# mLSTM values: which two of the four weight pages are split into the page pool and which two into the ring, exchanged

## The chip, the core and the metric

The kernel runs on one NeuronCore of a Trainium2 chip. The metric is the device time of one execution in microseconds; before the change it was 1633.11 us, the median of 3 runs (1631.96 to 1634.64). TensorE (PE) does the matmuls, VectorE (DVE), ScalarE (ACT) and GpSimd (POOL) the element work, and SyncE (SP) issues nearly all DMAs. Each engine works through its own instructions in the order in which the program put them, and waits on semaphores for the others.

## The reference

One decoder layer of 1024 rows and width 1024: three token mixers beside each other (stick-breaking attention, an mLSTM, cross-attention into 256 memory rows), a gated merge, and a ConvFFN. What the change touches is one column block of the input projection, the mLSTM's values (512 columns, `ml_v`):

```python
h = _rmsnorm(x, g_mix[l])
(sb_q, sb_k, sb_v, ml_q, ml_k, ml_v, ml_o, ml_i, ml_f, xa_q, gate_pre) = jnp.split(
    h @ w_in[l], offsets, axis=-1)
y_sb = _merge_heads(_stick_breaking_attention(
    _split_heads(sb_q, SB_HEADS), _split_heads(sb_k, SB_HEADS), _split_heads(sb_v, SB_HEADS)))
...
num = (jnp.einsum('bhts,bhsd->bhtd', s, vc)
       + w_inter[..., None] * jnp.einsum('bhvk,bhtk->bhtv', c_st, qc))
```

Here `vc` is one 128-row chunk of `ml_v`. All in fp32.

## The kernel before

**Products in three.** A product of fp32 operands is made of three matmuls of a faster format (`mm3`, lines 142, 143, 144): each operand is split into a high part, rounded by ACT (line 129), and a low part, the rest, subtracted on DVE (line 130). `wsplit` does this for a weight page of 128x1024: it loads the page into a `raw` tile by a DMA from SP (line 135) and splits it into two tiles, `hi` and `lo`.

**Where tiles live.** Tiles come from pools with a fixed number of slots for each tag; a new tile takes a slot over, and its first writer waits for the last reader of the tile that had it. Here these matter: `raw` (2 slots), `whi` and `wlo` (2 slots each, called the ring here), `pg` (16 slots, the page pool), and in PSUM the banks `pj`, `pv`, `z` and `tr`. A split goes into the ring unless `wsplit` is given another tag.

**The mLSTM's values.** `nat_chunks(1, ...)` makes eight tiles of 128 rows and 512 columns, each a sum over eight blocks k of the normalised input `hh`/`hl` (tiles `h`, the stationary operand) and four weight pages (the moving operand): page b serves k = 2b and 2b + 1, so a tile takes six matmuls for each of the pages 0, 1, 2, 3, in this order. All four pages are split once and stay for the eight tiles. Before, pages 0 and 1 lie in the ring and pages 2 and 3 in the page pool. The same generator makes the stick-breaking values (`which` 0): there it is given two pages that were split earlier (`ws=early`).

**What runs around it.** The stick-breaking attention goes over four pairs of heads p, each in twelve pieces: scores on PE (`sb_weights`, lines 394 and 395, bank `z`), two sigmoids on ACT (397, 398), a mask on POOL (403), scans on DVE (408) and a product (410); then transposes on PE (`sb_turn`, line 420, bank `tr`) with a copy on ACT (424 or 428), and products with the values (`sb_apply`, line 440, bank `pv`). Between the pieces PE runs chunks of a projection: those of the next pair's queries and keys while p < 3, and the mLSTM's values while p = 3. The queries and keys of a pair are six `pg` tiles, which are free when the pair's last scores are done. Behind the values come the gated projections (`seven`), whose weights are split in halves into `wlo` and `whi` in turn (`qring`), while `gx_part` makes their other operands, twelve `pg` tiles, from loads of `hn_d`.

**What sets the order.** The tile framework orders each engine's instructions by the program's order and by priorities; `tc.high_priority` in `nat_chunks` puts the loads and splits of the pages forward by a fixed offset (`SOON`), and what a slot's former reader allows decides where they land. So an exchange of slots moves rows on several engines.

Of the kernel before, what the change touches and what calls it, by code (L numbers as in the profile page):

```python
# [42 lines left out]
def tile_hybrid_layer(ctx: ExitStack, tc: tile.TileContext, xT, memT, vecs, w_t, w_n, w_kv, w_if,  # L43
# [24 lines left out]
    def T(shape, tag, dt=F32, bufs=None):  # L68
        pool = {"mw": mlp, "mst": mlp, "px": late[0], "sx": late[0]}.get(tag, sb)
        return pool.tile(shape, dt, tag=tag, name=nm(tag), bufs=bufs or BUFS[tag])  # L70
# [18 lines left out]
    def bank(tag):  # L89
        if tag in ("pj", "pv"):  # L90
            return ps.tile([P, HALF], F32, tag=tag, name=nm("ps_" + tag), bufs=2)
        if px1 is not None:
            if not spare.get(tag):
                t = two(tag)
                spare[tag] = [t[:, 1], t[:, 0]]
            return spare[tag].pop()
        return psx[0].tile([P, HALF], F32, tag=tag, name=nm("ps_" + tag), bufs=2)
# [4 lines left out]
    def hs(h):  # L102
        return slice(h * HALF, (h + 1) * HALF)

    def ts(t):
        return slice(t * P, (t + 1) * P)
# [21 lines left out]
    def split(src, hi, lo, eng=None):  # L128
        nc.scalar.activation(hi, src, AF.Copy)  # L129
        (eng or nc.vector).tensor_sub(lo, src, hi.bitcast(F32))  # L130

    def wsplit(src, tag=None, eng=None, raw=None):
        if raw is None:
            raw = T([P, S], "raw")
            nc.sync.dma_start(raw, src)
        hi = T([P, S], tag or "whi", F32R)
        lo = T([P, S], tag or "wlo", F32R)
        split(raw, hi, lo, eng)
        return hi, lo

    def mm3(out, lh, ll, rh, rl, start, stop, more=False):
        nc.tensor.matmul(out, lh, rh, start=start, stop=False, skip_group_check=more)  # L142
        nc.tensor.matmul(out, lh, rl, start=False, stop=False, skip_group_check=more)  # L143
        return nc.tensor.matmul(out, ll, rh, start=False, stop=stop, skip_group_check=more)  # L144
# [185 lines left out]

    def nat_chunks(which, consume, order=range(NCH - 1, -1, -1), ws=(), pauses=(3,)):
        with tc.high_priority(offset=SOON):
            ws = list(ws) + [wsplit(w_n[which, b], None if b < 2 or ws else "pg") for b in range(len(ws), 4)]
        for t in order:
            p = bank("pj")
            for k in range(KT):
                wh, wl = ws[k // 2]
                mm3(p, hh[k][:, ts(t)], hl[k][:, ts(t)], wh[:, hs(k % 2)], wl[:, hs(k % 2)],
                    k == 0, k == KT - 1)
                if k in pauses:  # L340
                    yield
            consume(t, p)
            yield
# [202 lines left out]
    def ev_sbv(t, p):  # L546
        if t % 2:
            sbv[t // 2] = T([P, 2, HALF], "pg")
        nc.scalar.activation(sbv[t // 2][:, t % 2, :], p, AF.Copy)

    vals = nat_chunks(0, ev_sbv, ws=early)
    for _ in range(2):
        next(vals)
# [46 lines left out]
    for p in range(4):  # L600
        now = st
        if p < 3:
            st, chunks = sb_qk(p + 1)
            chunks = itertools.chain(own, chunks())
            own = ()
        else:
            chunks = nat_chunks(1, ev_v, [0, 1, 2, 3, 7, 6, 5, 4], pauses=(1, 3, 5))
        for n, (rb, o) in enumerate(PIECES):
            g = sb_weights(p, now, rb, o)
            if len(turned) == 4:  # L610
                apply_all()
            if len(weights) == 2:
                turn_next()
            weights.append((p, rb, o, g))
            for _ in range((FIRST if p == 0 else NEXT)[n]):
                next(chunks, None)
        if p < 3:
            for _ in chunks:
                pass
# [470 lines left out]
    ws = [[None, None] for _ in range(4)]  # L1090
# [33 lines left out]
    for i in range(3 * KT):  # L1124
        b, n = i // KT, ORDER[i % KT]
# [512 lines left out]
```

## Time and profile before

| | us |
|---|---|
| median of the runs | 1633.11 |
| the profiled execution, its whole time | 1633.01 |
| its span (first to last instruction) | 1631.3 |
| granted TensorE clock, mean | 1.00 |
| mLSTM values, first to last matmul of theirs | 254.8 to 330.3 |

The timings of rows are from the profiled execution, counted from the start of the span; the whole time has 1.7 us more, which lie outside it. A row of the timeline gives start, duration, engine, line, operation, output and inputs with shapes, and in brackets how long the engine was idle before it and for whom; buffer numbers are left out there. PE's matmuls are pipelined, so that records overlap and a duration is longer than the step to the next start.

### The profile page before, as it was taken

To read this page: it belongs to the slowest core of one execution; us is meant where nothing else is said; L and a number is where in the kernel's file an instruction comes from. 1 tells how busy PE (TensorE), PEld (TensorE's weight loads), DVE (VectorE), ACT (ScalarE), POOL (GpSimd) and SP (SyncE) were. 2 spreads that over 40 slices of the span, in tenths; PEclk is the share of its full clock that TensorE was granted. 3 is DMA by queue.
4 is the path that set the end of the run, shared out by engine and by line. 5 is a ranking of instruction groups with operands and counts; after the bars stand their busy time and mean duration, and the time that the engine had idled before them with its cause. 6 is when DMAs were issued, how large, how long until landed. Compare 5 with 4: busy or idle time off the path is not lost.

```text
span 1631.3 us, 21183 instructions
## 1 busy us (share of the span) xinstructions
PE 1613.9 (99%) x7959; PEld 1322.4 (81%) x7959; DVE 1226.2 (75%) x1674; ACT 835.5 (51%) x1281; POOL 103.6 (6%) x175
## 2 busy tenths in 40 slices
PE   8999999999999999999999999999999999999999
PEld 4878888888878888888878888788888888888887
DVE  5658888859764666766586989987787777889764
ACT  4557777545554454656411456655555455543431
POOL 1022222020000010100000001100000000000000
PEclk9999999999999999999999999999999999999999
DMA  8420111324324665434884334432222221576131
GB/s 285 170 60 27 40 40 66 136 85 148 126 105 143 198 188 178 136 110 141 314 299 147 125 123 110 129 104 71 78 96 94 83 78 52 196 294 245 45 136 72
DMA packets 102082, 215.06 MB, mean 132 GB/s; under 512 B 13336, under 2 KB 37208, under 8 KB 101980
## 3 DMA queue, kind: packets, MB, share of 16 engines
q1 hardware_dynamic: 100396, 210.82, 38.1%
q0 software_dynamic: 1584, 2.88, 1.1%
q8 instruction: 63, 1.03, 0.3%
q14 instruction: 39, 0.32, 0.1%
HBM read 159.07 MB, written 54.61 MB: 131 GB/s over the span
## 4 chain that ended last, share of the span: by engine, by line
PE 92%; DMA 3%; DVE 3%; ACT 1%; issue 1%; SPq 0%; POOL 0%; DVEq 0%; ACTq 0%
PE ps_pj L142 13%; PE ps_pj L144 13%; PE ps_pj L143 13%; PE ps_pv L144 5%; PE ps_pv L142 5%; PE ps_pv L143 5%; PE ps_z L142 4%; PE ps_z L144 4%; PE ps_z L143 4%; PE ps_tr L142 4%; PE ps_tr L143 4%; PE ps_tr L144 4%; PE ps_pv L440 2%; PE ps_tr L420 2%; PE ps_z L215 1%; PE ps_z L395 1%
## 5 line engine op out<-in xcount | busy, mean ns | idle before, releaser
L143 PE MATMUL ps_pj<-h,whi 128*128 128x512 f32 x516 | 201.7, 391 | 0.0
L142 PE MATMUL ps_pj<-h,whi 128*128 128x512 f32 x436 | 173.9, 399 | 0.6 <-DVE U L1143 0.5
L129 ACT ACTIVATE whi<-raw 128x512 fp32r<-128x512 f32 (+1 forms) x99 | 81.2, 821 | 171.3 <-PE ps_pj L143 75.4
L144 PE MATMUL ps_pj<-h,wlo 128*128 128x512 f32 x352 | 137.6, 391 | 0.1
L848 DVE SCALAR_TENSOR_TENSOR y<-U,vec,y 128x1023 f32<-128x1023 f32 x88 | 112.6, 1280 | 8.4 <-ACT y L846 8.3
L143 PEld LDWEIGHTS ps_pj<-h,whi 128*128 128x128 f32 x516 | 97.1, 188 | 18.9 <-DVE U L276 0.2
L408 DVE TENSOR_TENSOR_SCAN U<-U 128x512 f32<-128x512 f32 (+3 forms) x96 | 92.8, 1009 | 22.1 <-POOL U L403 20.5
L142 PE MATMUL ps_pj<-pg,whi 128*128 128x512 f32 x268 | 104.7, 391 | 0.0
L144 PE MATMUL ps_pj<-pg,wlo 128*128 128x512 f32 x248 | 96.8, 390 | 0.0
L142 PEld LDWEIGHTS ps_pj<-h,whi 128*128 128x128 f32 x436 | 82.0, 188 | 17.6 <-issue 1.1
L144 PEld LDWEIGHTS ps_pj<-h,wlo 128*128 128x128 f32 x352 | 66.1, 188 | 14.7 <-DVE wlo L130 0.6
L129 ACT ACTIVATE whi<-pg 128x512 fp32r<-128x512 f32 (+1 forms) x54 | 43.7, 811 | 66.8 <-PE ps_z L143 18.7
L143 PE MATMUL ps_pv<-h,whi 128*128 128x512 f32 x190 | 74.0, 390 | 0.0
L143 PE MATMUL ps_pj<-pg,whi 128*128 128x512 f32 x188 | 73.4, 391 | 0.0
L130 DVE TENSOR_TENSOR wlo<-raw,whi 128x1024 fp32r<-128x1024 f32 x44 | 53.8, 1222 | 18.0 <-ACT whi L129 18.0
L846 ACT ACTIVATE y<-U,vec 128x1024 f32<-128x1024 f32 x44 | 54.6, 1242 | 20.4 <-DVE U L739 16.7
L144 PE MATMUL ps_pj<-h,whi 128*128 128x512 f32 x156 | 60.8, 390 | 0.0
L144 PE MATMUL ps_pv<-h,wlo 128*128 128x512 f32 x152 | 59.7, 392 | 0.0
L142 PE MATMUL ps_pv<-h,whi 128*128 128x512 f32 x150 | 59.0, 393 | 0.5 <-DVE U L739 0.5
L142 PEld LDWEIGHTS ps_pj<-pg,whi 128*128 128x128 f32 x268 | 50.3, 188 | 10.2
L144 PE MATMUL ps_tr<-pg,wlo 128*128 128x512 f32 x144 | 56.1, 389 | 0.0
L130 DVE TENSOR_TENSOR wlo<-raw,wlo 128x512 fp32r<-128x512 f32 x53 | 36.5, 688 | 26.0 <-ACT wlo L129 25.8
(508 smaller groups left out, 4485.8 us busy)
## 6 DMA issues: line engine op xcount, KB each, us to landing
raw<-in_w_t_dram SPq DMA_DIRECT2D x29, 512.0 KB
gate_d<-U SPq DMA_DIRECT2D x24, 512.0 KB
U<-gate_d SPq DMA_DIRECT2D x22, 512.0 KB
act_d<-y SPq DMA_DIRECT2D x22, 512.0 KB
pg<-in_w_t_dram SPq DMA_DIRECT2D x21, 512.0 KB
raw<-in_w_dn_dram SPq DMA_DIRECT2D x18, 512.0 KB
h<-act_d SPq DMA_DIRECT2D x14, 512.0 KB
raw<-in_w_br_dram SPq DMA_DIRECT2D x12, 512.0 KB
```

Source lines behind the costliest of these rows:

```text
L129: nc.scalar.activation(hi, src, AF.Copy)
L130: (eng or nc.vector).tensor_sub(lo, src, hi.bitcast(F32))
L142: nc.tensor.matmul(out, lh, rh, start=start, stop=False, skip_group_check=more)
L143: nc.tensor.matmul(out, lh, rl, start=False, stop=False, skip_group_check=more)
L144: return nc.tensor.matmul(out, ll, rh, start=False, stop=stop, skip_group_check=more)
L215: nc.tensor.matmul(pm[m], mg[k // 4][:, c], w[:, hs(kk)], start=(k == 0), stop=(k == KT - 1))
L395: nc.tensor.matmul(z[:, a, :w], qs[a][:, ts(rb)], kz[a][:, c], start=False, stop=True)
L408: nc.vector.tensor_tensor_scan(f[:, a, 1:w + 1], f[:, a, 1:w + 1], f[:, a, 1:w + 1], 1.0 if o == 0 else f[:, a, 0:1], op0=ALU.mult, op1=AL ...
L420: nc.tensor.transpose(pt[:, a, ts(j)], g[:, a, ts(j)], ident)
L440: nc.tensor.matmul(pv[64 * a:64 * a + 64, ts(rb % 4)], sbv[s // 2][:, s % 2, (2 * p + a) * 64:(2 * p + a + 1) * 64], wt[a][:, ts(j)], star ...
L846: nc.scalar.activation(out, u, AF.Identity, bias=bias, scale=taps[0])
L848: nc.vector.scalar_tensor_tensor(out[:, :S - s], u[:, s:], taps[s], out[:, :S - s], op0=ALU.mult, op1=ALU.add)
```

## The change

```diff
     def nat_chunks(which, consume, order=range(NCH - 1, -1, -1), ws=(), pauses=(3,)):
         with tc.high_priority(offset=SOON):
-            ws = list(ws) + [wsplit(w_n[which, b], None if b < 2 or ws else "pg") for b in range(len(ws), 4)]
+            ws = list(ws) + [wsplit(w_n[which, b], None if b > 1 else "pg") for b in range(len(ws), 4)]
```

For the mLSTM's values (no page given) pages 0 and 1 now go to the page pool and pages 2 and 3 to the ring. For the stick-breaking values, where b is only 2 and 3, both lines say the ring. No instruction is added or removed; the number of matmuls, splits and loads is the same.

The order of instructions changes on PE, DVE, ACT and SP; POOL's stays. In the rows below a tile's name ends in its number: `2426`/`2427` are the high and low part of page 0, `2432`/`2433` of page 1, `2438`/`2439` of page 2, `2444`/`2445` of page 3; `ps_pj_2448` is the first tile of values, `ps_z_2394` and `ps_z_2461` are the scores of the first two pieces of the last pair, and `xN` counts equal rows.

TensorE, at the start of the values, before:

```order
L395 MATMUL ps_z_2394<-pg_1871,pg_1867 128x128
L420 MATMUL ps_tr_2411<-ident,U_2313 128x128 x8
L142 MATMUL ps_pj_2448<-whi_2426,h_94 128x512
L143 MATMUL ps_pj_2448<-wlo_2427,h_94 128x512
L144 MATMUL ps_pj_2448<-whi_2426,h_102 128x512
L142 MATMUL ps_pj_2448<-whi_2426,h_95 128x512
L143 MATMUL ps_pj_2448<-wlo_2427,h_95 128x512
L144 MATMUL ps_pj_2448<-whi_2426,h_103 128x512
L142 MATMUL ps_pj_2448<-whi_2432,h_96 128x512
L143 MATMUL ps_pj_2448<-wlo_2433,h_96 128x512
```

The same place on TensorE now:

```order
L395 MATMUL ps_z_2394<-pg_1871,pg_1867 128x128
L142 MATMUL ps_pj_2448<-pg_2426,h_94 128x512
L440 MATMUL ps_pv_2324<-y_2356,pg_766 64x128 x2
L440 MATMUL ps_pv_2324<-y_2356,pg_636 64x128 x3
L420 MATMUL ps_tr_2411<-ident,U_2313 128x128 x8
L440 MATMUL ps_pv_2324<-y_2356,pg_636 64x128
L143 MATMUL ps_pj_2448<-pg_2427,h_94 128x512
L144 MATMUL ps_pj_2448<-pg_2426,h_102 128x512
L142 MATMUL ps_pj_2448<-pg_2426,h_95 128x512
L143 MATMUL ps_pj_2448<-pg_2427,h_95 128x512
L144 MATMUL ps_pj_2448<-pg_2426,h_103 128x512
L142 MATMUL ps_pj_2448<-pg_2432,h_96 128x512
```

Six products of the attention (L440) have come forward, one value matmul stands ahead of the eight transposes where none did, and the matmul on page 0's low part (2427) stands behind them. Further on the rest of the thirty products stands in five more groups between the value matmuls, scores and transposes; before they stood in two groups around the scores `ps_z_2495` (128x384), the third piece. The two lists of TensorE are alike again from `ps_z_2550` (the fourth piece) and the transposes behind it on, but for the tags of the pages.

DVE, the splits of the pages among the attention's work, before (from the scans and product of `U_2364` on):

```order
L408 SCALAR_TENSOR_TENSOR U_2363<-U_2363 128x512 x2
L410 TENSOR_TENSOR U_2364<-U_2364,U_2363 128x1024
L130 TENSOR_TENSOR wlo_2433<-raw_2430,whi_2432 128x1024
L130 TENSOR_TENSOR pg_2439<-raw_2436,pg_2438 128x1024
L368 TENSOR_TENSOR pg_1870<-ps_pj_2268,pg_1868 64x512
```

And now:

```order
L408 SCALAR_TENSOR_TENSOR U_2363<-U_2363 128x512 x2
L410 TENSOR_TENSOR U_2364<-U_2364,U_2363 128x1024
L130 TENSOR_TENSOR pg_2427<-raw_2424,pg_2426 128x1024
L130 TENSOR_TENSOR pg_2433<-raw_2430,pg_2432 128x1024
L368 TENSOR_TENSOR pg_1870<-ps_pj_2268,pg_1868 64x512
```

The low part of page 0 was made some twenty rows earlier before; now it has page 1's place, page 1 has page 2's, and page 2 stands five rows further down, behind the scans of `U_2466`, with page 3 two rows behind it. On ACT the high parts follow suit: page 0's behind the second sigmoid of `U_2364` and ahead of the two copies of line 428, page 1's among the copies of the keys (364 to 367), pages 2 and 3 around the second sigmoid of `U_2467`. On SP the load of page 2 (`raw_2436`), which takes over page 0's raw slot, is moved behind a store of the attention's output.

DVE at the end of the values, where the weights of the first gated projection (`raw_3158`) are split into the ring; `pg_3019` is one of the operands that `gx_part` makes. Before:

```order
L795 TENSOR_TENSOR U_3096<-U_3096,U_3095 128x1024
L130 TENSOR_TENSOR wlo_3164<-raw_3158,wlo_3164 128x512
L130 TENSOR_TENSOR whi_3181<-raw_3158,whi_3181 128x512
L130 TENSOR_TENSOR pg_3019<-U_3096,pg_3018 128x1024
L130 TENSOR_TENSOR wlo_3207<-raw_3201,wlo_3207 128x512
```

And now:

```order
L795 TENSOR_TENSOR U_3096<-U_3096,U_3095 128x1024
L130 TENSOR_TENSOR pg_3019<-U_3096,pg_3018 128x1024
L130 TENSOR_TENSOR wlo_3164<-raw_3158,wlo_3164 128x512
L130 TENSOR_TENSOR whi_3181<-raw_3158,whi_3181 128x512
L130 TENSOR_TENSOR wlo_3207<-raw_3201,wlo_3207 128x512
```

`pg_3019` has come forward by two rows, as the ring's slots are read last now. ACT has the same exchange with `pg_3018`. On SP the loads of the raw tiles that take over the value pages' slots in the page pool (`pg_3160`, `pg_3203`, `pg_3244`) stand where they stood, but wait for the matmuls of pages 0 and 1 instead of those of pages 2 and 3.

## The prediction, made before the changed kernel was run

> **What bounds the kernel now.** I read the page's first and fourth parts, then TensorE's list of waits around the changed code, then the timelines of TensorE, ACT, DVE and SP there.
>
> ```profile
> PE 1613.9 (99%) x7959; PEld 1322.4 (81%) x7959; DVE 1226.2 (75%) x1674; ACT 835.5 (51%) x1281; POOL 103.6 (6%) x175
> PE 92%; DMA 3%; DVE 3%; ACT 1%; issue 1%; SPq 0%; POOL 0%; DVEq 0%; ACTq 0%
> ```
>
> TensorE (PE) is busy 99% of the span and carries 92% of the chain that ended last. So a microsecond that PE stands still in the middle is a microsecond of the result, and what another engine gains is worth nothing unless PE waited for it. In the stretch from 225 to 360 us, which holds the mLSTM values and the start of the gated projections behind them, PE's list of waits has one entry:
>
> ```profile
> PE ps_pj L143 <- DVE wlo L130: 0.9, 1, 0.9
> ```
>
> This is the most that the change could win there. It sits at the first value tile, pj_2448:
>
> ```profile
> 253.99 1.09 PE L420 MATMUL ps_tr<-ident,U 128*128 128x128 f32 x8
> 254.84 0.48 PE L142 MATMUL ps_pj<-whi,h 128*128 128x512 f32 x1
> ...
> 256.31 0.40 PE L142 MATMUL ps_pj<-whi,h 128*128 128x512 f32 x1
> 257.57 0.50 PE L143 MATMUL ps_pj<-wlo,h 128*128 128x512 f32 x1 [0.86 <-DVE wlo L130]
> 257.91 0.40 PE L144 MATMUL ps_pj<-whi,h 128*128 128x512 f32 x1
> 258.15 0.40 PE L142 MATMUL ps_pj<-whi,h 128*128 128x512 f32 x1
> ...
> 259.55 0.28 PE L394 MATMUL ps_z<-pg,pg 128*128 128x256 f32 x1
> ```
>
> PE ran the eight transposes and seven value matmuls (page 0 and the first of page 1), then stood 0.86 us until page 1's low part was there. Starts matter here, not durations: records overlap, and a 512-wide matmul starts every 0.23 us.
>
> **Page 0 and page 1, now in the page pool.** Page 0's split was done early:
>
> ```profile
> 227.94 1.06 ACT L129 ACTIVATE whi<-raw 128x1024 fp32r<-128x1024 f32 x1
> ```
>
> In the page pool it has to wait for a slot that the scores of the pair before still read, and the order now puts it behind them: on ACT ahead of the two L428 copies, on DVE behind the product U_2364 (L410). The rows of that place:
>
> ```profile
> 253.05 0.88 ACT L428 ACTIVATE hf<-ps_tr 128x384 f32<-128x384 f32 x2
> 253.79 1.08 ACT L129 ACTIVATE whi<-raw 128x1024 fp32r<-128x1024 f32 x1
> 255.16 1.23 DVE L410 TENSOR_TENSOR U<-U,U 128x1024 f32<-128x1024 f32 x1
> 256.30 1.22 DVE L130 TENSOR_TENSOR wlo<-raw,whi 128x1024 fp32r<-128x1024 f32 x1
> 257.43 1.22 DVE L130 TENSOR_TENSOR pg<-raw,pg 128x1024 fp32r<-128x1024 f32 x1
> ```
>
> Nothing ahead of 253.05 on ACT or 256.30 on DVE becomes later, so page 0's high part takes 253.05 to 254.13 and its low part takes DVE's place at 256.30, where page 1's low part was; page 1's takes 257.43. PE's L143 on page 0's low part therefore starts at 257.57, the very time at which the old wait ended. Ahead of it PE now has one value matmul (254.18, behind ACT's 254.13), five L440 products, the eight transposes (they need the tr bank, which L428 frees about 1 us later than now, at 254.9; they start at about 255.3) and one more product. That is done at about 256.3, so the wait grows to about 1.2 us. At 257.57 PE has done six value matmuls fewer than before and six products more. What a product costs:
>
> ```profile
> 261.27 0.48 PE L144 MATMUL ps_pj<-pg,h 128*128 128x512 f32 x1
> 261.68 0.87 PE L440 MATMUL ps_pv<-y,pg 128*64 128x128 f32 x10
> 262.51 0.44 PE L394 MATMUL ps_z<-pg,pg 128*128 128x384 f32 x1
> ...
> 263.15 0.34 PE L395 MATMUL ps_z<-pg,pg 128*128 128x384 f32 x1
> 263.42 0.54 PE L440 MATMUL ps_pv<-y,pg 128*64 128x128 f32 x5
> ...
> 266.41 0.44 PE L420 MATMUL ps_tr<-ident,U 128*128 128x128 f32 x2
> 266.60 0.47 PE L394 MATMUL ps_z<-pg,pg 128*128 128x512 f32 x1
> ```
>
> Five rows of the program are ten records, so a product is two. From 263.42 to 266.41 stand 50 records: 0.06 us each, 0.12 a product. Term one: 6 x 0.23 - 6 x 0.12 = **+0.7 us**.
>
> **More changes between kinds of matmul.** Behind 257.57 the products stand in five groups now, and in two before. A change costs: from a score matmul to products 263.15 to 263.42, 0.27 where the step was 0.18; back from products to a wide matmul:
>
> ```profile
> 312.90 1.04 PE L440 MATMUL ps_pv<-y,pg 128*64 128x128 f32 x16
> 313.87 0.50 PE L142 MATMUL ps_pj<-whi,h 128*128 128x512 f32 x1
> 314.21 0.39 PE L143 MATMUL ps_pj<-wlo,h 128*128 128x512 f32 x1
> ```
>
> The second wide one comes 0.34 behind the first and not 0.23, and 0.04 is lost ahead. So 0.09 + 0.04 + 0.11 = 0.24 a group, three groups more: **+0.7 us**. If the groups cost nothing because the next wait covers them, this term is 0; I take it whole, as the next waits are short.
>
> **Page 2 and page 3, now in the ring.** Their raw tiles take over the two raw buffers from pages 0 and 1, so page 2's load moves from 231.24 to the place where page 3's stands:
>
> ```profile
> 231.24 0.33 SPq L135 DMA_DIRECT2D raw<-in_w_n_dram  x1
> ...
> 257.55 0.33 SPq L135 DMA_DIRECT2D raw<-in_w_n_dram  x1
> 258.68 5.70 SPq L688 DMA_DIRECT2D raw<-in_w_t_dram  x2
> 260.21 0.60 ACT L397 ACTIVATE U<-ps_z 128x512 f32<-128x512 f32 x1 [0.46 <-PE ps_z L395]
> 260.92 1.06 ACT L129 ACTIVATE pg<-raw 128x1024 fp32r<-128x1024 f32 x1
> 262.67 1.35 DVE L130 TENSOR_TENSOR pg<-raw,pg 128x1024 fp32r<-128x1024 f32 x1
> 262.50:263.00 0.50, 0.50 (x4) 0.49 (x4) 0.50 (x2) 0.50 (x1) 0.41 (x1) 1.00 0.01 0
> ```
>
> The first load was used at 260.92, and the last column of the window behind 262.5 (GB/s) shows that both had landed by then. The same two places now carry pages 2 and 3. PE's scores z_2461 move from 259.55 to about 260.6 (eleven value matmuls and a product lie ahead of them from 257.57, where eight did). ACT's L397 follows at 261.3, page 2's high part from 261.8 to 262.85: the load, there at 260.9, has 0.9 us to spare. PE reaches that matmul at about 262.65 and waits 0.2 us. Page 2's low part is on DVE by 264.85 (behind the scans, which wait for that L397); PE is there at 264.75 and waits 0.1. Against these stand some 0.2 us that PE lost ahead of the scores at 262.51 before. Queued behind the waiting matmul are the scores z_2495, and ACT's L397 of them and all of pair 3's chain behind that; they become about 1.5 us later, as everything does. Net **+0.1 us**; with one more ACT split (1.06) in front of either, +1.2; fully hidden, -0.2. I take the walk through the rows, 0.1. Sum at z_2550: 266.60 becomes about 268.1, **+1.5 us**. From there the rows are the same, ACT and DVE have idle time, PE has none, and the delay stays.
>
> **The end of the values.** The ring is read last now, so the first split of the next stage finds its slot later.
>
> ```profile
> 325.81 0.39 PE L143 MATMUL ps_pj<-wlo,h 128*128 128x512 f32 x1
> 326.23 0.64 ACT L129 ACTIVATE wlo<-raw 128x512 fp32r<-128x512 f32 x1 [0.48 <-PE ps_pj L143]
> ...
> 328.53 0.39 PE L143 MATMUL ps_pj<-pg,h 128*128 128x512 f32 x1
> ...
> 328.83 1.23 DVE L130 TENSOR_TENSOR pg<-U,pg 128x1024 fp32r<-128x1024 f32 x1
> ...
> 330.34 0.39 PE L142 MATMUL ps_tr<-h,wlo 128*128 128x512 f32 x1
> ...
> 330.79 0.39 PE L144 MATMUL ps_tr<-h,wlo 128*128 128x512 f32 x1
> ```
>
> In old times: ACT started 0.03 us behind the end of the slot's last reader (326.20). That reader becomes the matmul at 328.53, so ACT runs 328.95 to 329.6, ahead of PE's 330.34. The low part now stands on DVE behind the tile that takes 328.83 to 330.06, and with 0.69 us is ready at about 330.7; PE wants it at 330.79. I take **0**; a late DVE would show at once, with 0.7 (one such low part) as the upper end. The four raw pages that reuse the value pages' slots can be loaded 2.7 us sooner; no PE wait in this stretch is on them, so they bring nothing.
>
> **Sum.** 0.7 + 0.7 + 0.1 + 0 = +1.5 us on the profiled execution's own 1633.01: 1634.5. It stands 0.10 under the median of the runs, 1633.11, so **1634.6**. A measurement of this kernel can tell about 0.2% (3.3 us) from no change.
>
> **Rivals.**
> (a) Nothing moves PE, within 0.4 us: needs term two hidden and the waits at -0.2, leaving 0.5, or a restart before 257.57. For it: the restart falls on the old time. Against: six matmuls are still owed. 1633.1 to 1633.5.
> (b) The wait is gone, as page 0 and 1 no longer wait for the ring: -0.9, 1632.2. Against: DVE's place at 256.30 hangs on L410, not on the ring.
> (c) Slower: page 2's load becomes the wait. It has 0.9 us to spare; each further us passes to PE through the matmul on its high part, behind which scores and products queue. At 263.6, 2.7 us later than the row's 260.92, it makes 1.8 more and the total +3.3, 1636.4; later is slower beyond what can be told. Against: both loads were over by 262.5, and no other load is issued there.
> (d) The waits slow the clock. The window behind the 0.86 us wait (third column from its end: granted clock):
>
> ```profile
> 257.50:258.50 1.00, 0.93 (x4) 0.78 (x5) 1.00 (x2) 0.97 (x3) 0.00 (x0) 1.00 0.00 0
> ```
>
> The clock stands at 1.00, and matmuls came 0.24 apart at once; a wait of 1.2 us is not far from that. If the clock halved until the scores at 260.6, the eleven value matmuls would take 11 x 0.23 = 2.5 us more: 1637.1. [...]
>
> **Chances and range.** Forecast (+0.5 to +3.2) 0.74, (a) 0.12, (b) 0.05, (c) 0.07, (d) 0.02. The upper end is 1.5 + 1.1 (an ACT split) + 0.7 (the end) = +3.3, with the spread of the runs, 1636.9; the lower takes in (a) and most of (b), 1632.3. Faster by over 0.2%: 0.02, since no row offers more than 0.9 us; slower by over 0.2%: (c), (d) and the top of the forecast, 0.10; within: 0.88.
>
> **What will show it.** Right: page 0's splits near 253 and 256.3, a PE wait of about 1.2 us that ends at 257.6 on DVE L130, short ones on ACT L129 and DVE L130 near 262.9 and 264.9, z_2550 near 268.1, the values' last matmul about 1.5 us later, no wait at the first ps_tr matmul. Wrong: a restart ahead of 257.5, a wait on DMA raw, or a delay that shrinks between 268 and 330.

## The result, and the profile after

| | before | changed |
|---|---|---|
| median of 13 runs each, us | 1635.17 | 1638.27 |
| lowest and highest | 1631.96 to 1639.06 | 1634.47 to 1641.67 |
| the profiled execution, whole time | 1633.01 | 1641.67 |

The changed kernel is slower by 0.2%: ratio 1.0023, 95% interval [1.0013, 1.0032], which is 2.1 to 5.2 us. The forecast was +1.5 us. Of the distance between 1634.6 and 1638.27 us, 2.1 us come from the kernel before itself, whose 13 runs have a median 2.1 us above that of the first three; the other 1.6 us are what the change cost beyond the forecast, 3.1 and not 1.5. The profiled execution of the changed kernel was also the slowest of its 13, so the 8.66 us between the two profiles are more than the change: part of them is chance, and has to be told apart.

The page of the changed kernel has its busy times and the chain almost as before:

```profile
PE 1619.6 (99%) x7959; PEld 1324.2 (81%) x7959; DVE 1225.8 (75%) x1674; ACT 835.0 (51%) x1281; POOL 104.9 (6%) x175
PE 90%; DMA 3%; DVE 3%; issue 2%; ACT 1%; POOL 0%; SPq 0%; POOLq 0%; DVEq 0%; ACTq 0%
```

DVE and ACT did the same work in the same time. TensorE (PE) has 5.7 us more "busy" for the same 7959 matmuls, which no wait can do; that is a first hint at its clock. TensorE's list of waits in the stretch from 225 to 360 us, which had one entry of 0.9 us before:

```profile
PE ps_tr L142 <- ACT wlo L129: 1.7, 1, 1.7
PE ps_pj L143 <- DVE pg L130: 0.7, 1, 0.7
PE ps_tr L144 <- DVE wlo L130: 0.6, 1, 0.6
PE ps_pj L142 <- ACT pg L129: 0.3, 1, 0.3
```

The second and the fourth are those that the prediction had at the first value tile. The first and the third stand at the first gated projection, behind the values, where it had none. Laid beside the old trace, instruction for instruction, the starts of TensorE are 0.1 us early at 200 us, 1.7 late at 266.6 (the fourth piece's scores), 4.5 late at 331, 5.5 at 540, 7.2 at 860 and 8.7 at the end. So there are three places. The first, the timeline of the middle in the changed kernel, TensorE's rows with ACT's and DVE's splits of page 2:

```profile
254.02 0.50 PE L142 MATMUL ps_pj<-pg,h 128*128 128x512 f32 x1 [0.28 <-ACT pg L129]
254.45 0.87 PE L440 MATMUL ps_pv<-y,pg 128*64 128x128 f32 x10
255.25 1.09 PE L420 MATMUL ps_tr<-ident,U 128*128 128x128 f32 x8
256.27 0.43 PE L440 MATMUL ps_pv<-y,pg 128*64 128x128 f32 x2
257.43 0.50 PE L143 MATMUL ps_pj<-pg,h 128*128 128x512 f32 x1 [0.72 <-DVE pg L130]
...
258.69 0.39 PE L142 MATMUL ps_pj<-pg,h 128*128 128x512 f32 x1
259.01 0.43 PE L440 MATMUL ps_pv<-y,pg 128*64 128x128 f32 x2
259.37 0.50 PE L143 MATMUL ps_pj<-pg,h 128*128 128x512 f32 x1
259.71 0.39 PE L144 MATMUL ps_pj<-pg,h 128*128 128x512 f32 x1
...
261.81 1.05 ACT L129 ACTIVATE whi<-raw 128x1024 fp32r<-128x1024 f32 x1
...
262.90 0.50 PE L142 MATMUL ps_pj<-whi,h 128*128 128x512 f32 x1
...
263.61 1.36 DVE L130 TENSOR_TENSOR wlo<-raw,whi 128x1024 fp32r<-128x1024 f32 x1
...
265.02 0.50 PE L143 MATMUL ps_pj<-wlo,h 128*128 128x512 f32 x1
...
268.25 0.48 PE L394 MATMUL ps_z<-pg,pg 128*128 128x512 f32 x1
```

The restart on page 0's low part comes at 257.43, the old 257.57 less the 0.13 by which this execution was early; page 2's matmuls at 262.90 and 265.02 have no wait in the list, but each starts 0.05 us behind the end of the split that it needs (262.86 on ACT, 264.97 on DVE). From the restart to the fourth piece's scores the old trace took 9.03 us and this one 10.82. The second place, the end of the values, DVE, ACT and TensorE of the changed kernel in order of time:

```profile
313.64 1.23 DVE L789 TENSOR_TENSOR U<-U,U 128x1024 f32<-128x1024 f32 x1 [3.08 <-DMA U<-hn_d]
...
330.97 1.22 DVE L795 TENSOR_TENSOR U<-U,U 128x1024 f32<-128x1024 f32 x1
332.22 1.06 ACT L129 ACTIVATE pg<-U 128x1024 fp32r<-128x1024 f32 x1 [2.41 <-DVE U L795]
333.18 0.61 ACT L129 ACTIVATE wlo<-raw 128x512 fp32r<-128x512 f32 x1
333.31 1.22 DVE L130 TENSOR_TENSOR pg<-U,pg 128x1024 fp32r<-128x1024 f32 x1 [1.12 <-ACT pg L129]
333.85 0.50 PE L142 MATMUL ps_tr<-h,wlo 128*128 128x512 f32 x1 [1.68 <-ACT wlo L129]
334.45 0.69 DVE L130 TENSOR_TENSOR wlo<-raw,wlo 128x512 fp32r<-128x512 f32 x1
335.19 0.50 PE L144 MATMUL ps_tr<-h,wlo 128*128 128x512 f32 x1 [0.61 <-DVE wlo L130]
```

The same in the kernel before:

```profile
309.59 1.22 DVE L789 TENSOR_TENSOR U<-U,U 128x1024 f32<-128x1024 f32 x1 [0.72 <-DMA U<-hn_d]
...
326.48 1.22 DVE L795 TENSOR_TENSOR U<-U,U 128x1024 f32<-128x1024 f32 x1
327.62 0.69 DVE L130 TENSOR_TENSOR wlo<-raw,wlo 128x512 fp32r<-128x512 f32 x1
```

Read the chain from the top. In the first of `gx_part`'s two calls the subtraction L789 waited 3.08 us for a load of `hn_d` and not 0.72; in the second call L789 waited 1.30 and not 0.57. Everything behind them in DVE's queue moved, and the second call's L795, which makes the last tile, ran 4.5 us later than before, while TensorE was 1.7 late. In the new order the tile's split (ACT pg, DVE pg) stands ahead of the first weight split on both engines. From the end of L795 to TensorE's L144 it is 332.19 to 335.19, 3.0 us, as in all six executions with the new order shown below, and so the late load arrives at TensorE. In the old order the first weight split stood ahead of that tile's split on both engines; ACT's half of it waits for no `hn_d`, and DVE's half had only L795 itself ahead of it.

The third place is the clock. The window view has granted clock in the third column from the end:

```profile
335.50:336.00 0.50, 0.50 (x3) 0.42 (x2) 0.50 (x2) 0.34 (x1) 0.00 (x0) 0.86 0.39 156
336.00:337.00 1.00, 1.00 (x4) 0.71 (x3) 1.00 (x3) 0.00 (x0) 0.00 (x0) 0.50 1.07 309
```

The clock was halved from 335.86 for 3.41 us, and matmuls came 0.43 apart instead of 0.23; once more from 1052.66, behind a wait of 2.1 us for a load of `in_w_up` that the kernel before has too, without the halving. That is about 1.6 us each. Another 1.9 us came at 818 to 850, in the merge, as waits on DVE (L1141 and L1143), and about 1.2 us of all this was made up elsewhere.

### The profile page after: what moved, and what is told of

It reads as the page before. It is cut to its first block, busy times and chain, and to the rows that moved or that the text cites. A ratio compares the mean times of both kernels' runs of the same rounds, so it can differ in the third digit from the quotient of the medians.

```text
span 1640.0 us, 21185 instructions
## 1 busy us (share of the span) xinstructions
PE 1619.6 (99%) x7959; PEld 1324.2 (81%) x7959; DVE 1225.8 (75%) x1674; ACT 835.0 (51%) x1281; POOL 104.9 (6%) x175
## 4 chain that ended last, share of the span: by engine, by line
PE 90%; DMA 3%; DVE 3%; issue 2%; ACT 1%; POOL 0%; SPq 0%; POOLq 0%; DVEq 0%; ACTq 0%
PE ps_pj L142 12%; PE ps_pj L143 12%; PE ps_pj L144 12%; PE ps_pv L144 6%; PE ps_pv L142 6%; PE ps_pv L143 6%; PE ps_z L142 4%; PE ps_tr L144 4%; PE ps_tr L142 4%; PE ps_tr L143 4%; PE ps_z L144 4%; PE ps_z L143 4%; PE ps_pv L440 1%; PE ps_tr L420 1%; DMA pg<-in_w_o_dram 1%
## 5 line engine op out<-in xcount | busy, mean ns | idle before, releaser
L144 PE MATMUL ps_pj<-h,wlo 128*128 128x512 f32 x352 | 137.5, 391 | 0.1
L144 PE MATMUL ps_pj<-pg,wlo 128*128 128x512 f32 x248 | 96.7, 390 | 0.0
L144 PEld LDWEIGHTS ps_pj<-h,wlo 128*128 128x128 f32 x352 | 66.1, 188 | 14.6 <-DVE wlo L130 0.6
L130 DVE TENSOR_TENSOR wlo<-raw,whi 128x1024 fp32r<-128x1024 f32 x44 | 53.9, 1225 | 17.2 <-ACT whi L129 17.1
L144 PE MATMUL ps_pj<-h,whi 128*128 128x512 f32 x156 | 61.1, 392 | 0.0
L144 PE MATMUL ps_pv<-h,wlo 128*128 128x512 f32 x152 | 59.6, 392 | 0.0
L397 ACT ACTIVATE U<-ps_z 128x1024 f32<-128x1024 f32 (+3 forms) x48 | 39.1, 814 | 33.6 <-PE ps_z L395 25.2
L144 PE MATMUL ps_tr<-pg,wlo 128*128 128x512 f32 x144 | 56.1, 389 | 0.0
```

Source lines behind the costliest of these rows:

```text
L397: nc.scalar.activation(f[:, :, 1:w + 1], z[:, :, :w], AF.Sigmoid, scale=-0.125)
```

## The experiments

All are single-core kernels of the same program. "Middle" is what TensorE lost between 200 and 267 us against the old trace, "end" what it lost between 300 and 331 us, each from one profiled execution; the ratio is from timed runs of the kernel and of the kernel before on the same chip.

### The changed kernel again

No edit. The question is what of the 8.66 us comes back.

> The changed kernel a second time, to see which of its waits come again. Theory A (the order makes the waits): the delay at the fourth piece's scores is again +1.5 to +2.0 us against the kernel before; at the first matmul of the gated projections TensorE waits between 0 and 2.5 us, as much as the load of hn_d is late, since the last tile of gx_part now stands ahead of the first weight split; the ratio is 1.001 to 1.003. Rival B (one unlucky execution): the delay at the fourth piece comes again, the wait at the gated projections does not (under 0.3 us) with hn_d just as late, and the ratio is under 1.0015.

Measured: median 1637.40 against 1634.81 us, ratio 1.0019 [1.0010, 1.0028]; the profiled execution had no halved clock. Middle +1.8, end +1.7 (DVE L789 again waited 3.07 us for `hn_d`), the merge +3.0. So the middle and the end wait come back, and the halving does not.

### Pages 0 and 3 in the ring

```diff
-wsplit(w_n[which, b], None if b > 1 else "pg")
+wsplit(w_n[which, b], None if which == 0 or b in (0, 3) else "pg")
```

> Pages 0 and 3 in the ring, 1 and 2 in the page pool: page 0 is split early as before, and the first weight split of the gated projections stands ahead of gx_part's last tile as before, though the ring's second slot is read last. Theory A: the one wait of 0.9 us on page 1's low part stays, no delay at the fourth piece (under 0.4 us), no wait at the first gated matmul, ratio 0.999 to 1.001. Rival C (it is the ring being read by the values' last matmuls that costs): a wait of 0.5 us or more in the first two gated products, ratio 1.001 or more.

Measured: 1633.23 against 1634.81 us, ratio 0.9993 [0.9984, 1.0002]. Middle 0.0, end 0.0; TensorE has the old wait of 0.8 us on page 1's low part. With page 0 in the ring the middle loss is gone.

### Pages 1 and 2 in the ring

```diff
-wsplit(w_n[which, b], None if b > 1 else "pg")
+wsplit(w_n[which, b], None if which == 0 or b in (1, 2) else "pg")
```

> Pages 1 and 2 in the ring, 0 and 3 in the page pool: page 0 late at 256 as in the changed kernel, but pages 1 and 2 have the places that pages 0 and 1 had; the ring slot of the first gated split is free 2.7 us sooner than in the changed kernel, while gx_part's last tile still stands ahead of that split. Theory A: the wait on page 0's low part ends at 257.5, and the delay at the fourth piece is +0.5 to +1.3 us; the wait at the first gated matmul comes if hn_d is late and not otherwise, 0 to 2.5 us; ratio 1.0005 to 1.0025. Rival C (the late ring slot, not the order, makes the second wait): no wait there, whatever hn_d does.

Measured: 1636.27 against 1634.81 us, ratio 1.0010 [1.0000, 1.0021]. Middle +0.3, which is below the +0.5 to +1.3 expected, and end +1.8. The middle:

```profile
257.71 0.50 PE L143 MATMUL ps_pj<-pg,h 128*128 128x512 f32 x1 [0.69 <-DVE pg L130]
...
267.01 0.48 PE L394 MATMUL ps_z<-pg,pg 128*128 128x512 f32 x1
```

Page 0's low part stands behind L410 as in the changed kernel, and the restart has the same wait; yet only 0.3 us is lost by the fourth piece's scores. What differs behind the restart is page 2: its high part is split at 254.91 here and at 261.81 in the changed kernel, and the products behind the restart stand in one group and not in five. So page 0's late split alone is not the 1.8 us of the changed kernel. The end:

```profile
328.68 1.22 DVE L795 TENSOR_TENSOR U<-U,U 128x1024 f32<-128x1024 f32 x1
329.93 1.06 ACT L129 ACTIVATE pg<-U 128x1024 fp32r<-128x1024 f32 x1 [2.41 <-DVE U L795]
330.89 0.61 ACT L129 ACTIVATE wlo<-raw 128x512 fp32r<-128x512 f32 x1
331.56 0.50 PE L142 MATMUL ps_tr<-h,wlo 128*128 128x512 f32 x1 [0.66 <-ACT wlo L129]
332.90 0.50 PE L144 MATMUL ps_tr<-h,wlo 128*128 128x512 f32 x1 [0.61 <-DVE wlo L130]
```

Here the ring's slots come free 2.7 us sooner than in the changed kernel, and the wait is there all the same: ACT's `wlo` waits for nothing, it stands behind `pg`, and `pg` waits for L795. So it is the order on ACT and DVE, not the slot.

### The changed kernel with the old order at the end

The last tile of `gx_part` (its subtraction and split) is put behind the first weight split; the pages stay changed. This goes one row further than the order of the kernel before, where the subtraction stood ahead of that split.

```diff
-    for j in range(2):
-        gx_part(j)
...
+    rest = gx_part(1)
...
+    go(1)
+    with tc.issue_after(low[0].ins):
+        gx_last(*rest)
+    go(2)
```

(`low[0]` is the DVE instruction of the first weight split.)

> The changed kernel with gx_part's last tile (line 795 and its split) put behind the first weight split of the gated projections on ACT and DVE; the pages' slots as in the changed kernel. Theory A: delay at the fourth piece as in the changed kernel, +1.5 to +2.0 us, and no wait over 0.4 us at the first gated matmul even where hn_d is late; ratio 1.000 to 1.0015, below that of the changed kernel. Rival C (the late ring slot): the wait at the first gated matmul stays at 1 us or more. Rival B: no difference from the changed kernel.

Measured: 1635.96 against 1634.81 us, ratio 1.0012 [1.0003, 1.0022]. Middle +1.8, end 0.0, although DVE waited 2.65 us for `hn_d` at the old L789. What is left is the middle.

### The kernel before, made late

Whether lateness alone makes the end wait, and why `hn_d` lands late:

```diff
-                wh, wl = ws[k // 2]
+                wh, wl = ws[k // 2]; [nc.tensor.matmul(p, hh[k][:, ts(t)], wh[:, hs(0)], start=True, stop=True) for _ in range(7 if (which, t, k) == (1, 1, 0) else 0)]
```

> The kernel before with seven extra matmuls (7 x 0.23 = 1.6 us) at the start of the second value tile, whose sums are overwritten; nothing else moves. It makes TensorE late by what the changed pages made it late, and keeps the old order at the end of the values. Theory A (the end wait needs the new order and loads of hn_d that land late): TensorE is +1.6 us from 272.3 on, and there is no wait at the first gated matmul, since the first weight split stands ahead of the last tile of gx_part. Whole time +1.6 us, ratio 1.0010. On why hn_d lands late: if it is only the later place of the loads in time, the load that DVE L789 waits for takes 5 to 6 us from issue here too (3.6 before); if it is something that the changed pages bring, it takes 3.6. Rival (lateness alone makes the wait): 0.6 us or more at the first gated matmul, +2.5 us or more. On the later waits on DVE for pg L1141 and U L1143 (2 to 3 us in three kernels with the new order, 0.5 before): they come back if a late TensorE is enough for them.

Measured: 1634.42 against 1632.81 us, ratio 1.0008 [0.9999, 1.0017]. TensorE was 1.6 us later behind the seven matmuls, the end +0.0, and the merge added 0.2. DVE L789 waited 2.99 us for `hn_d`:

```profile
312.84 1.23 DVE L789 TENSOR_TENSOR U<-U,U 128x1024 f32<-128x1024 f32 x1 [2.99 <-DMA U<-hn_d]
...
329.45 1.22 DVE L795 TENSOR_TENSOR U<-U,U 128x1024 f32<-128x1024 f32 x1
330.59 0.68 DVE L130 TENSOR_TENSOR wlo<-raw,wlo 128x512 fp32r<-128x512 f32 x1
```

L795 was as late as in the changed kernel's second execution, but TensorE came at 331.86 for the low part that DVE had ready at 331.27. So this late load, with the old order, cost nothing, and the changed pages are not what makes it late.

### The kernel before with the new order at the end

```diff
     def qring(src, soon=SOON):
         t = pair(turn(0, ("whi", "wlo")))
+        if behind and cyc[0] < 3:
+            with tc.high_priority(offset=soon), tc.issue_after(behind[0].ins), tc.issue_after(behind[1].ins):
+                split(src, *t)
+            return t
...
-        split(bu, *gd["t4"][j])
+        last = split(bu, *gd["t4"][j])
+        if j:
+            behind.extend(last)
```

(`split` now returns its two instructions; `behind` holds the two instructions of that last split for j = 1.)

> The kernel before with one exchange: the last tile of gx_part is split ahead of the first weight of the gated projections, on ACT and DVE, as the changed kernel has it. The pages stay where they were. Theory A: TensorE is on time, so hn_d lands in 3.6 us as before, DVE L795's successor ends by 327.7, the low part of the weight is ready 3.0 us later, 330.7, and TensorE wants it at 330.79: a wait of 0 to 0.3 us; ratio 1.0000. Rival (the order alone costs the wait): 1.2 us or more at the first gated matmul, ratio 1.0008 or more.

Measured: 1634.09 against 1632.81 us, ratio 1.0007 [0.9997, 1.0017]; middle -0.1, end +1.5:

```profile
310.74 1.23 DVE L795 TENSOR_TENSOR U<-U,U 128x1024 f32<-128x1024 f32 x1 [2.74 <-DMA U<-hn_d]
...
327.26 1.22 DVE L801 TENSOR_TENSOR U<-U,U 128x1024 f32<-128x1024 f32 x1
```

(Lines are six further down in this kernel: L795 is the old L789, L801 the old L795.) My expectation of no wait fell with its condition: I had `hn_d` landing on time here, as nothing ahead of it was changed, and it landed 2 us late. In the trace the order alone is enough, in an execution whose loads are late; the ratio's interval still takes in no change.

### Both edits on the kernel before

The two edits above together.

> Both edits on the kernel before: seven extra matmuls in the second value tile (their sums are overwritten) and the exchange at the end. Theory A, with hn_d late because of its place in time: +1.6 us from the matmuls and a wait of 1 to 2 us at the first gated matmul, together about +3 us, ratio 1.0015 to 1.0020, as the changed kernel. If hn_d is late only with the changed pages: a wait of at most 0.3 us, ratio 1.0010. Rival (two independent sums): the total of the two kernels with one edit each.

Measured: 1639.01 against 1632.81 us, ratio 1.0034 [1.0021, 1.0047], from six runs only. In the trace the matmuls cost 1.6, the end 1.9, a stretch at half clock about 1.6 (an estimate: the mean clock of this execution is 0.999, and a halved window cost that much in the changed kernel). The first two are what was expected; the ratio is above them, and five of the six runs show a mean clock below 1.000. Whether that is chance, these six runs cannot tell.

### The value pages' splits put forward, in both kernels

```diff
     def nat_chunks(which, consume, order=range(NCH - 1, -1, -1), ws=(), pauses=(3,)):
-        with tc.high_priority(offset=SOON):
+        with tc.high_priority(offset=60 if which else SOON):
```

In the kernel before:

> The kernel before, where the splits of the mLSTM's value pages are put forward by 60 instead of 40. Page 1's low part then stands on DVE ahead of the product L410 of U_2364 and not behind it, so it should be ready about 1.2 us sooner, and the wait of 0.86 us at 257.57 goes. In exchange the first scores of the last pair stand behind seven value matmuls. If the end of the wait is all that counts: -0.9 us, ratio 0.9995. Rival (the later scores and the later product give it back): 0 to +1 us, ratio 1.0000 to 1.0006, with a new wait on ACT or DVE behind 258.

Measured: 1632.62 against 1632.81 us, ratio 0.9998 [0.9989, 1.0007]. The wait of 0.86 us is gone, and the middle gained 0.3 us, not 0.9: the rest was given back in smaller steps behind it.

In the changed kernel:

> The changed kernel, where the splits of the mLSTM's value pages are put forward by 60 instead of 40, so that page 0's and page 1's low parts stand on DVE ahead of the product L410 of U_2364. Theory A for the middle (the restart was pinned at 257.5 by DVE's place behind that product): the wait of 0.72 us on page 0's low part goes, and TensorE at the fourth piece's scores stands at +0.5 us or less of the kernel before, not at +1.8. The end keeps its new order, so the waits at the first gated matmuls stay, together 0.9 to 1.7 us. Ratio 1.0006 to 1.0013. Rival (the middle term comes from the pool's slots, which the scores of the pair before hold): the wait comes back on ACT and the middle stays at +1.5 us or more, ratio 1.0019.

Measured: 1635.49 against 1633.78 us, ratio 1.0009 [0.9999, 1.0020]; middle -0.3, end +1.7. DVE now has the split ahead of the product:

```profile
251.60 1.22 DVE L130 TENSOR_TENSOR pg<-raw,pg 128x1024 fp32r<-128x1024 f32 x1
252.74 2.45 DVE L408 TENSOR_TENSOR_SCAN U<-U 128x512 f32<-128x512 f32 x2
255.11 1.20 DVE L130 TENSOR_TENSOR pg<-raw,pg 128x1024 fp32r<-128x1024 f32 x1
256.22 1.22 DVE L410 TENSOR_TENSOR U<-U,U 128x1024 f32<-128x1024 f32 x1
```

Page 0's low part is made at 251.60 and not at 256.15, so a slot of the page pool was free by then: the middle loss came from the places of the splits in the order, not from the slots. The edit moves the splits of all four pages (page 2's high part comes at 256.73 and not at 261.81), so it does not tell page 0's share from page 2's; the kernel with pages 1 and 2 in the ring does.

In the changed kernel with the old order at the end as well:

> The changed kernel with both edits: the value pages split earlier (60 instead of 40) and the last tile of gx_part behind the first weight split. If the two terms, middle and end, are all that the change costs: within 0.5 us of the kernel before throughout, no wait at the first gated matmul, ratio 1.0000 to 1.0003. Rival (the pages in the other pools cost something else, later loads or stores for one): ratio 1.0008 or more.

Measured: 1632.82 against 1633.78 us, ratio 0.9996 [0.9988, 1.0005]. Middle -0.25, end 0.0. With both terms undone, and the pages still exchanged, nothing measurable is left of the change.

### All of them side by side

| kernel | pages in the ring | new order at the end | wait for `hn_d` at the first L789 | middle + end, us | ratio |
|---|---|---|---|---|---|
| changed | 2, 3 | yes | 3.08 | 1.8 + 2.9 | 1.0023 |
| changed, again | 2, 3 | yes | 3.07 | 1.8 + 1.7 | 1.0019 |
| pages 1, 2 | 1, 2 | yes | 1.71 | 0.3 + 1.8 | 1.0010 |
| changed, split earlier | 2, 3 | yes | 2.43 | -0.3 + 1.7 | 1.0009 |
| before, new order | 0, 1 | yes | 2.74 | -0.1 + 1.5 | 1.0007 |
| before, both edits | 0, 1 | yes | 2.75 | 1.6 (matmuls) + 1.9 | 1.0034 |
| changed, old order | 2, 3 | no | 2.65 | 1.8 + 0.0 | 1.0012 |
| before, made late | 0, 1 | no | 2.99 | 1.6 (matmuls) + 0.0 | 1.0008 |
| pages 0, 3 | 0, 3 | no | 1.02 | 0.0 + 0.0 | 0.9993 |
| before, split earlier | 0, 1 | no | 3.23 | -0.3 + 0.1 | 0.9998 |
| changed, both undone | 2, 3 | no | 0.71 | -0.3 + 0.0 | 0.9996 |

The end costs 1.5 to 2.9 us in all six executions with the new order, and at most 0.1 in the five without it, whether `hn_d` was late or not. The wait at the first L789 does not give its size (3.08 and 3.07 stand beside 2.9 and 1.7), as the second call's loads vary too. What gives it is the second call's L795: set against TensorE, it started 2.8, 1.6, 1.8, 1.6, 1.5 and 1.9 us later than in the kernel before in the six rows with the new order, and the end lost 2.9, 1.7, 1.8, 1.7, 1.5 and 1.9. With the old order it was 1.9 late in the kernel made late and 2.3 in the kernel before with earlier splits, and the end lost 0.0 and 0.1.

Times 1634 us, the ratios give +3.8, 3.1, 1.6, 1.5, 1.1, 5.6, 2.0, 1.3, -1.1, -0.3 and -0.7 us: within about 1 us of the two terms' sum in ten of eleven rows, the exception being the row with six runs. Such an interval is about 1.5 us wide to either side. The timed runs alone set the two series of the changed kernel, the changed kernel with the old order and the kernel with both edits apart from the kernel before; the interval of pages 1 and 2 touches 1, those of the other six take it in, and there the terms rest on one trace each.

## Why the prediction was wrong

**The step that failed is "the end of the values", taken as 0 with 0.7 at most.** Its rows were read rightly: the low part would stand behind the tile that DVE takes at 328.83, ready at about 330.7 where TensorE wants it at 330.79. The text even said that a late DVE would show at once. What it took wrongly is that DVE would be on time, as in the one trace of before. The end lost 2.9 and 1.7 us in the two traces of the changed kernel. DVE's time there hangs on the loads of `hn_d`, and in that execution they were early: the wait at the first L789 was 0.72 us, in nine of the eleven others 1.7 to 3.2 us, in kernels of both kinds. With 0.1 us of slack, such a place is priced by how far its feeder can be late, and I had bounded it by one instruction (0.7), which was no bound. The old order had 2.5 us of slack at this place (ready at 328.31, the end of DVE's first `wlo`, wanted at 330.79), and it was this slack that the change spent.

**The middle, +1.5, was right in mechanism and 0.3 short.** Of what was to show it, page 0's splits came at 252.91 and 256.15, the restart at the old time on DVE L130 behind L410, the fourth piece's scores at 268.25; only the wait ahead of the restart was 0.72 and not 1.2, as TensorE was busy a little longer in front of it, which does not move the restart; six value matmuls were owed and six products done, 1.38 - 0.72 = 0.7, as predicted (term one). The short waits on page 2 came where they were forecast, at 262.90 and 265.02, though the list shows no idle time there: the ends of matmul records are modelled, and the products' records in front reach over the gap. By 0.06 us a record these products (12 records from 262.08, four from 264.61) end at 262.80 and 264.85, so the waits are 0.1 to 0.2 us each, an estimate.

The mis-sized term is the change between kinds of matmul, taken as 0.24 a group: it and the waits were to cost 0.8 together, and 1.79 - 0.66 = 1.1 us was left for them, at most 0.38 for each of three more groups. The group at 259.01, where nothing is waited for, shows the price: from the wide matmul at 258.69 to the next at 259.37 it is 0.68 us, of which 0.23 is the usual step and 0.12 the product, so 0.33, and the step behind it (259.37 to 259.71) is 0.34 and not 0.23, 0.11 more. With pages 1 and 2 in the ring the same restart was followed by one group fewer than before, and 0.66 fell to 0.31, 0.35 for a group. It is not one number, though: with the earlier splits the changed kernel has five groups in all, three more than before, and no wait of 0.86; at 0.38 a group it would lose 0.3, and it gained 0.3.

The earlier splits undid the whole middle, which shows that the places of the splits were the cause: page 0's behind L410, and page 2's at 261.81. That the groups come with page 2 is read from the two orders, the changed one and the one with pages 1 and 2 in the ring, and was not tested alone. The prediction's other reason for page 0's place, that its slot was still read, did not bind: with the earlier splits the slot was free.

**Rival (d), a halved clock, was given 0.02**, my estimate: it asked for 1.2 us of waiting in the middle, the clock stood at 1.00 behind the old wait of 0.86 us, and no row of before showed what length of wait would do more. In the middle the clock stayed whole, 1.00 behind the wait of 0.72 us. The halving happened elsewhere and by chance: once behind the new end wait and once behind the wait for `in_w_up` in one profiled execution, not in the second one. In the timed runs the mean clock does not part the kernels: it is below 1.000 in 7 of 13 of the changed kernel, in 6 of 11 of its second series, and in 15 of the 33 of the kernel before beside that. Among the runs whose mean clock is 1.000 alone, the second series has a median of 1637.40 (5 runs) against 1633.47 (18 runs), 3.9 us. So it widens the spread, and it is not what made the median slower.

**Rivals (a), (b), (c)** did not come: TensorE moved, the restart did not come sooner, and page 2's load was not waited for in the changed kernel.

**The base**: three runs put the kernel before at 1633.11, 13 at 1635.17. The range had "the spread of the runs" of those three in it, which was too little. On 1635.17 the same upper end, 3.8 us above, would have been 1639.0, above the measured 1638.27: it took the base and the end together to leave the range.

Open: why the load of `hn_d` takes 3.5 to 4.5 us in four executions and 5.2 to 5.9 in eight. In the trace such a load lands in 16 parts; in the changed kernel 14 of the one that DVE L789 waited for had landed by 311.15 us, the last two at 312.98 and 313.55. What held these two was not found. Nor was it found what sets the loss in the merge (0.2 to 3.0 us at 800 to 860 us, without the halving): the two largest, 3.0 and, without its halved window, 2.9, belong to the changed kernel's second execution and to the kernel before with the new order, but the changed kernel with both terms undone lost 2.5 there as well and was not slower in its median. The six executions with the new order lost 0.8 to 3.0 us there, five of them 1.9 or more, and four of the five others at most 1.1; whether the order has a part in it was not tested.

## What to carry to other kernels

An exchange of slots also exchanges the order on the engines that fill them; look at each place where a row was moved in front of another, and ask what the moved row waits for, not only how long it runs. Slack at such a place is worth nothing or everything depending on how far its feeder varies, and one profiled execution shows one draw of a DMA's time: a slack of 0.1 us behind a load should be priced at the load's spread, with a second trace if there is one.

## What the runs showed of the hardware that I had not expected

In the changed kernel's trace the granted clock is 0.50 from 335.86 to 339.27, from 1052.66 to 1056.07, 3.41 us each, and once more from 1639.75, behind the last matmul. From the first of these starts to the last it is 1303.89 us and from the second 587.09; in the kernel before the trace's record of the clock has 1.00 from 12.23 (its first matmuls come 0.85 us apart up to there and 0.43 behind it) to 1630.14, 1617.92 us, and 0.50 from there. These three lengths are 382, 172 and 474 times 3.4133 us, within 0.02 us. So in each trace I counted windows of this length back from the halved one behind the last matmul, and added up TensorE's idle time in each (gaps between the rows of its timeline, whose ends are modelled for matmuls). The longest wait is that of TensorE's list of waits:

| execution | longest wait, us | largest idle time in one window, us | next window |
|---|---|---|---|
| changed | 2.1 | 2.05 and 2.01 | clock 0.50, both |
| before, new order | 2.1 | 2.07 | clock 0.50 |
| before, both edits | 2.7 | 1.93 | half clock (mean of the execution 0.999) |
| before, split earlier | 1.8 | 1.78 | half clock (matmuls 0.43 apart) |
| changed, both undone | 1.7 | 1.73 | full (matmuls 0.23 apart) |
| pages 0, 3 | 1.8 | 1.69 | full |
| changed, split earlier | 1.6 | 1.59 | full |
| before and the four others | 1.2 to 2.4 | 1.21 to 1.48 | full |

(Behind the first 15 us, in which the kernel starts.) In these twelve executions a halved window came behind 1.78 us or more of idle time in one window and none behind 1.73 or less, while the longest wait alone does not part them: one of 2.4 us stands in a row without a halved window. No run was made to test this. The timelines of the two neighbours, the kernel before with earlier splits and the changed kernel with both terms undone, at the same wait:

```profile
1043.08 0.50 PE L144 MATMUL ps_pv<-h,whi 128*128 128x512 f32 x1 [1.78 <-DMA whi<-in_w_up_dram]
...
1044.51 0.63 PE L143 MATMUL ps_pv<-pg,whi 128*128 128x512 f32 x1
1044.93 0.63 PE L142 MATMUL ps_pj<-h,whi 128*128 128x512 f32 x1
```

```profile
1044.05 0.50 PE L144 MATMUL ps_pv<-h,whi 128*128 128x512 f32 x1 [1.74 <-DMA whi<-in_w_up_dram]
...
1045.31 0.40 PE L143 MATMUL ps_pv<-pg,whi 128*128 128x512 f32 x1
1045.55 0.39 PE L142 MATMUL ps_pj<-h,whi 128*128 128x512 f32 x1
```

That accounts for the chance: behind the wait of 2.1 us on `in_w_up` the clock was 0.50 in the changed kernel, where 2.05 us fell into one window, and 1.00 in the kernel before, where the same 2.1 us lay across two with at most 1.41 in one. A halved window of 3.41 us cost about 1.6 us here, an estimate from the matmuls that came 0.43 us apart and not 0.23, so a wait of 1.8 to 2.1 us that fell into one window cost nearly twice its length.
